# Issuing the value products of two attention heads together, into the two halves of TensorE's columns, in a two-layer hybrid backbone

## The chip, the cores and the metric

The kernel runs on one core of a Trainium2 chip. The metric is the device time of one execution in microseconds (us), as the median of several executions. All data is in HBM at the start and the output is in HBM at the end. Engines are called as in the profile: PE is TensorE's matrix multiply, PEld its weight load, DVE is VectorE, ACT is ScalarE, POOL is GpSimd, SP is SyncE, which here issues nearly all DMAs.

## What is computed

The reference is two layers of a backbone over 256 context and 256 latent tokens, width 1024, all in float32. Each layer mixes tokens in four parallel groups of four heads or channels (an mLSTM, latent attention "mla", windowed attention "swa", a linear recurrence) behind one input projection and before one output projection. Layer 0 then has a dense SwiGLU, layer 1 a mixture of eight experts, two per token. A conditioning vector gives shifts, scales and gates (`ada_w`). The part that matters here is the attention of the two middle groups:

```python
def block_attention(q, k, v):          # mla: 4 heads, blocks of 128 queries
    s = jnp.einsum('bhqd,bhkd->bhqk', qblk, k).astype(F32) * scale
    p = jax.nn.softmax(s, axis=-1)
    return jnp.einsum('bhqk,bhkd->bhqd', p.astype(v.dtype), v)
...
def swa_mixer(...):                    # swa: 4 heads, 2 groups of keys and values, window 128, a sink
    p = softmax_with_sink(s, sink_h[:, :, None, None, None]).astype(vl.dtype)
    o = (jnp.einsum('bhgnqk,bhnkd->bhgnqd', p[..., :KL], vb)
         + jnp.einsum('bhgnqk,bhkd->bhgnqd', p[..., KL:], vc))
```

Context queries see 256 keys, latent queries see 512. Layer 0 has outputs for all 512 tokens, layer 1 for the 256 latent ones only. Each head has 64 values per token.

## The kernel before, in words

Time goes through the program in this order: the start with the first modulation; the mixer of layer 0 (input projection, mLSTM, attention); its output projection (`w_out`); the dense SwiGLU (`ffn`); the mixer of layer 1; its `w_out`; the experts (`moe`), which stream their weights in 333 loads of 1024 KB.

**Attention** is one list of items, built by `items` (L819): one item is one head and one block `t` of 128 queries, with `w` keys (256 for t = 0, 1 and 512 for t = 2, 3). The four mla heads and then the four swa heads make 32 items in layer 0 (`full`) and 16 in layer 1 (t = 2, 3 only). The list runs head by head, and the blocks within a head. `attend` (L824) goes over the list as a software pipeline. In iteration i it issues

- `scores` (L831) of item i: the product of queries and keys into a bank of PSUM (L835; for swa a mask is added by a product with the identity, L838), then the softmax: maximum and sign on DVE (L842, L844), exponential with its sum on ACT (L849), reciprocal on DVE (L853), normalisation on POOL (L854);
- `turn` (L857) of item i - 3: PE transposes the probabilities P in pieces of 128 x 128 (L860), and ACT (odd i, L863) or DVE (even i, L865) copies them out of PSUM as PT;
- `value` (L868) of item i - 4: `w / 128` products add up one head's output. The weights are the head's values (128 keys x 64), the moving operand is PT (128 keys x 128 queries), and the result has 64 partitions.

```python
c, p = h // 2, 64 * (h % 2)
...
nc.tensor.matmul(ob[p:p + 64, t * 128:(t + 1) * 128], lhsT=q["head"][2](s), rhs=q["PT"][:, s * 128:(s + 1) * 128],
                 start=(s == 0), stop=(s == w // 128 - 1))
```

An even head writes partitions 0 to 63 of bank `ob`, that is, it uses columns 0 to 63 of the array; an odd head uses columns 64 to 127 and the other partitions of the same bank. After the last block of an odd head, `emit_y` (L588) splits the pair's output into a high and a low part for `w_out`.

**What stands beside it.** `mixer` (L1258) advances the mLSTM generator once per iteration of `attend` in layer 0 and twice in layer 1: decays (L735, L738 on PE, L742 on ACT), products (L752 on PE, L757 on DVE), values (L770 on PE). The mLSTM's end (L801 to L816, with transposes on PE at L809) waits in the program until attention is done. In layer 0 `tick` also lets a background generator `ada` go on, which loads `ada_w` (L335, tile `adaw`, on SP) and multiplies it (L347, L358). The tile framework orders each engine's instructions from these by priority and readiness, so a group of products can be cut by other work.

**Buffers.** P and PT come from one pool tag `t2` (34 buffers in layer 0, 33 in layer 1). The score and transpose banks have the tag A (4 banks); the banks of `value` and of the mLSTM have the tag B (3 banks in layer 0, 4 in layer 1).

A matrix product of plain float32 operands is one instruction in the program and two records in the trace, each with its own weight load.

Of the kernel before, what the change touches and what calls it, by code (L numbers as in the profile page):

```python
# [130 lines left out]
class Net:  # L131
# [685 lines left out]

    def items(self, i0, full, heads, sink=None):

        return [dict(i0=i0, h=h, head=hd, t=t, w=256 if t < 2 else 512, sink=sink, last=t == 3)  # L820
                for h, hd in enumerate(heads) for t in ((0, 1, 2, 3) if full else (2, 3))]

    def attend(self, items, full):

        nc, mp = self.nc, self.mp
        V = nc.vector
        c0 = 0 if full else 256
        obs = {}

        def scores(q):  # L830
            qT, kT, _ = q["head"]  # L831
            t, w, h, sink = q["t"], q["w"], q["h"], q["sink"]
            b = self.bank("A")
            loc = sink is not None and t >= 2
            nc.tensor.matmul(b[:, :w], lhsT=qT[:, t * 128:(t + 1) * 128], rhs=kT[:, :w], start=True, stop=not loc)  # L835
            if loc:
                o = 5 - t
                nc.tensor.matmul(b[:, o * 128:(o + 1) * 128], lhsT=self.ident,  # L838
                                 rhs=self.C("swa_m0" if t == 2 else "swa_m1"), start=False, stop=True)
            nm = mp.tile([128, 4], F32, name="nm", tag="nm", bufs=8)  # L840
            m, sm = nm[:, 0:1], nm[:, 1:2]
            V.tensor_reduce(m, b[:, :w], axis=AX.X, op=OP.max)  # L842
            if sink is None:
                V.tensor_scalar(m, m, -1.0, None, op0=OP.mult)  # L844
            else:
                sk = sink[:, h:h + 1]
                V.tensor_scalar(m, m, sk, -1.0, op0=OP.max, op1=OP.mult)
            P = q["P"] = self.T2("P")
            nc.scalar.activation(P[:, :w], b[:, :w], AF.Exp, bias=m, accum_out=sm)  # L849
            if sink is not None:  # L850
                nc.scalar.activation(nm[:, 2:3], m, AF.Exp, bias=sk)
                V.tensor_tensor(sm, sm, nm[:, 2:3], op=OP.add)
            V.reciprocal(sm, sm)  # L853
            nc.gpsimd.tensor_scalar(P[:, :w], P[:, :w], sm, 1.0, op0=OP.mult, op1=OP.mult)  # L854

        def turn(q, i):
            w = q["w"]  # L857
            b = self.bank("A")
            for s in range(0, w, 128):
                nc.tensor.transpose(b[:, s:s + 128], q["P"][:, s:s + 128], self.ident)  # L860
            pt = q["PT"] = self.T2("PT")
            if i % 2:
                nc.scalar.activation(pt[:, :w], b[:, :w], AF.Copy)  # L863
            else:
                V.tensor_copy(pt[:, :w], b[:, :w])  # L865

        def value(q):
            i0, h, t, w = q["i0"], q["h"], q["t"], q["w"]  # L868
            c, p = h // 2, 64 * (h % 2)
            if (i0, c) not in obs:  # L870
                obs[i0, c] = self.bank("B")
            ob = obs[i0, c]
            for s in range(w // 128):
                nc.tensor.matmul(ob[p:p + 64, t * 128:(t + 1) * 128], lhsT=q["head"][2](s), rhs=q["PT"][:, s * 128:(s + 1) * 128],  # L874
                                 start=(s == 0), stop=(s == w // 128 - 1))
            if q["last"] and p:
                self.emit_y(i0 + c, ob, c0)

        n = len(items)
        for i in range(n + 4):  # L880
            if i < n:
                scores(items[i])
            if 0 <= i - 3 < n:
                turn(items[i - 3], i)
            if i >= 4:
                value(items[i - 4])
            yield

    def rope(self, dst, x, parts, t0, nf, tmp):
# [980 lines left out]
```

## Time and profile before

| | us |
|---|---|
| median of 3 runs | 2014.39 (2011.48 to 2016.26) |
| the profiled execution | 2016.45 |
| its span, first to last instruction | 2014.7 |
| PE busy | 1876.2 (93% of the span), 10051 records |
| DVE, ACT, POOL busy | 918.4, 767.2, 85.3 |

The profile's busy times are those of one execution. A busy PE is not one at its peak: each record lasts from its start to a modelled end, and records overlap, so what a group of products costs is read from the distance between starts. [...] Attention lies between about 202 and 369 us (layer 0) and between 956 and 1028 us (layer 1).

### The profile page before, as it was taken

To read this page: it belongs to the slowest core of one execution; us is meant where nothing else is said; L and a number is where in the kernel's file an instruction comes from. 1 tells how busy PE (TensorE), PEld (TensorE's weight loads), DVE (VectorE), ACT (ScalarE), POOL (GpSimd) and SP (SyncE) were. 2 spreads that over 40 slices of the span, in tenths; PEclk is the share of its full clock that TensorE was granted. 3 is DMA by queue.
4 is the path that set the end of the run, shared out by engine and by line. 5 is a ranking of instruction groups with operands and counts; after the bars stand their busy time and mean duration, and the time that the engine had idled before them with its cause. 6 is when DMAs were issued, how large, how long until landed. Compare 5 with 4: busy or idle time off the path is not lost.

```text
span 2014.7 us, 26293 instructions
## 1 busy us (share of the span) xinstructions
PE 1876.2 (93%) x10051; PEld 1235.0 (61%) x10051; DVE 918.4 (46%) x1678; ACT 767.2 (38%) x1331; POOL 85.3 (4%) x121
## 2 busy tenths in 40 slices
PE   6999999989999999888988999789999989899988
PEld 3777455678888888667686886454454444444443
DVE  3556334453433434675567965333324333333323
ACT  3745433253223233654547854232322222323221
POOL 0210111000000000210100000000000000000000
PEclk8999899989999999888998989999999989999999
DMA  8543356412323233331045969999999989999997
GB/s 276 181 136 110 126 193 204 152 63 95 96 93 96 92 97 92 102 85 48 1 166 201 363 225 380 405 408 409 401 376 349 410 321 380 409 401 372 409 405 300
DMA packets 190958, 474.73 MB, mean 236 GB/s; under 512 B 18596, under 2 KB 81768, under 8 KB 190824
## 3 DMA queue, kind: packets, MB, share of 16 engines
q1 hardware_dynamic: 190456, 472.76, 64.2%
q8 instruction: 81, 1.33, 0.3%
q14 instruction: 53, 0.43, 0.1%
q10 hardware_dynamic: 368, 0.21, 0.0%
HBM read 471.88 MB, written 1.05 MB: 235 GB/s over the span
## 4 chain that ended last, share of the span: by engine, by line
PE 63%; DMA 5%; DVE 5%; ACT 3%; issue 2%; DVEq 0%; SPq 0%; ACTq 0%
PE bankA L1572 16%; PE bankA L528 7%; PE bankA L527 7%; PE bankA L526 7%; PE bankA L1567 6%; PE bankA L1568 5%; PE bankA L1566 5%; DMA w<-in_moe_w_dram 5%; DVE wl L210 2%; ACT wh L209 1%; PE bankA L1531 1%; PE bankA L1602 1%; PE bankA L835 1%; PE bankB L874 1%; PE bankA L1714 1%
## 5 line engine op out<-in xcount | busy, mean ns | idle before, releaser
L210 DVE TENSOR_TENSOR wl<-w,wh 128x1024 fp32r<-128x1024 f32 x222 | 263.9, 1222 | 257.8 <-ACT wh L209 245.7
L209 ACT ACTIVATE wh<-w 128x1024 fp32r<-128x1024 f32 x222 | 225.7, 1053 | 156.7 <-DMA w<-in_moe_w_dram 126.7
L1572 PE MATMUL bankA<-w,xl 128*32 128x256 f32 (+3 forms) x1784 | 228.4, 452 | 15.0 <-DMA w<-in_moe_w_dram 15.0
L1572 PEld LDWEIGHTS bankA<-w,xl 128*32 128x32 f32 (+1 forms) x1784 | 83.7, 124 | 134.3 <-issue 96.5
L1567 PE MATMUL bankA<-wl,xe 128*128 128x512 f32 x336 | 140.7, 419 | 19.2 <-DVE wl L210 19.2
L1566 PE MATMUL bankA<-wh,xe 128*128 128x512 f32 x336 | 129.0, 425 | 14.8 <-ACT wh L209 14.4
L1568 PE MATMUL bankA<-wh,xe 128*128 128x512 f32 x336 | 136.5, 406 | 0.0
L1572 PE MATMUL bankA<-w,ut 128*32 128x256 f32 (+1 forms) x792 | 116.4, 490 | 0.8 <-DMA w<-in_moe_w_dram 0.8
L1650 ACT ACTIVATE sg<-bankA 128x512 f32<-128x512 f32 (+2 forms) x45 | 23.1, 533 | 196.6 <-PE bankA L1572 159.1
L1566 PEld LDWEIGHTS bankA<-wh,xe 128*128 128x128 f32 x336 | 61.7, 194 | 54.4 <-ACT wh L209 28.8
L1567 PEld LDWEIGHTS bankA<-wl,xe 128*128 128x128 f32 x336 | 65.9, 196 | 44.0 <-DVE wl L210 29.7
L1567 PE MATMUL bankA<-wl,uh 128*128 128x512 f32 x168 | 68.8, 409 | 9.4 <-DVE wl L210 9.4
L1653 DVE TENSOR_TENSOR sg<-bankA,sg 128x512 f32<-128x512 f32 (+2 forms) x45 | 27.0, 612 | 108.7 <-PE bankA L1572 89.0
L1572 PEld LDWEIGHTS bankA<-w,ut 128*32 128x32 f32 (+1 forms) x792 | 36.6, 122 | 63.9 <-issue 56.5
L1568 PEld LDWEIGHTS bankA<-wh,xe 128*128 128x128 f32 x336 | 66.0, 196 | 13.9
L528 PE MATMUL bankA<-uh,w2l 128*128 128x512 f32 x176 | 70.2, 399 | 0.0
L528 PE MATMUL bankA<-hh,wgl 128*128 128x512 f32 x176 | 70.2, 399 | 0.0
L527 PE MATMUL bankA<-hl,wgh 128*128 128x512 f32 x176 | 69.3, 394 | 0.0
L527 PE MATMUL bankA<-ul,w2h 128*128 128x512 f32 x176 | 69.3, 394 | 0.0
L526 PE MATMUL bankA<-uh,w2h 128*128 128x512 f32 x176 | 69.0, 392 | 0.0
L526 PE MATMUL bankA<-hh,wgh 128*128 128x512 f32 x176 | 69.0, 392 | 0.0
L347 PE MATMUL bankC<-adaw,stat 128*32 128x512 f32 x352 | 67.3, 617 | 1.5 <-DMA adaw<-in_ada_w_dram 1.5
(489 smaller groups left out, 3679.1 us busy)
## 6 DMA issues: line engine op xcount, KB each, us to landing
w<-in_moe_w_dram SPq DMA_DIRECT2D x286, 1024.0 KB, 10.1
adaw<-in_ada_w_dram SPq DMA_DIRECT2D x96, 512.0 KB, 4.8
xT<-in_moe_w_dram SPq DMA_DIRECT2D x47, 1024.0 KB, 9.2
wa<-in_ffn_w_dram SPq DMA_DIRECT2D x22, 512.0 KB
wg<-in_ffn_w_dram SPq DMA_DIRECT2D x22, 512.0 KB, 3.5
w<-in_ffn_w_dram SPq DMA_DIRECT2D x20, 512.0 KB, 3.4
wo<-in_w_out_dram SPq DMA_DIRECT2D x12, 512.0 KB, 3.5
wU<-in_w_in_dram SPq DMA_DIRECT2D x4, 512.0 KB
```

The costliest lines, as they stand in the source:

```text
L209: nc.scalar.activation(h, src, AF.Copy)
L210: ins = nc.vector.tensor_tensor(lo[:, q:q + m], src, h.bitcast(F32), op=OP.subtract)
L347: mark(nc.tensor.matmul(b[32 * q:32 * q + 32], lhsT=self.stat[:, j], rhs=rs[j][:, h * 512:(h + 1) * 512], start=(i == 1), stop=(i == 7)))
L526: t.matmul(out, lhsT=whi, rhs=hhi, start=start, stop=False)
L527: t.matmul(out, lhsT=whi, rhs=hlo, start=False, stop=False)
L528: t.matmul(out, lhsT=wlo, rhs=hhi, start=False, stop=stop)
L1566: t.matmul(b, lhsT=x[0], rhs=hi[:, c], start=start, stop=False)
L1567: t.matmul(b, lhsT=x[0], rhs=lo[:, c], start=False, stop=False)
L1568: t.matmul(b, lhsT=x[1], rhs=hi[:, c], start=False, stop=stop)
L1572: t.matmul(out[0][n * s:n * s + n, 0:h], lhsT=x, rhs=w[:, s * h:(s + 1) * h], start=start, stop=stop)
L1650: nc.scalar.activation(g[:, 0:h], b[:, 0:h], AF.Silu)
L1653: V.tensor_tensor(g[:, 0:h], b[:, 0:h], g[:, 0:h], op=OP.mult)
```

## The change

The list of items goes by pairs of heads (0 and 1, then 2 and 3), within a pair by blocks, and within a block by the two heads. `value` takes both heads of a pair at once, in odd iterations only: it issues their products in turns, one of the lower and one of the upper half of the columns. So the first item of a pair has its products one iteration later than before, the second one as before.

```diff
-        return [dict(i0=i0, h=h, head=hd, t=t, w=256 if t < 2 else 512, sink=sink, last=t == 3)
-                for h, hd in enumerate(heads) for t in ((0, 1, 2, 3) if full else (2, 3))]
+        return [dict(i0=i0, h=h, head=heads[h], t=t, w=256 if t < 2 else 512, sink=sink, last=t == 3)
+                for c in range(2) for t in ((0, 1, 2, 3) if full else (2, 3)) for h in (2 * c, 2 * c + 1)]
...
-        def value(q):
-            i0, h, t, w = q["i0"], q["h"], q["t"], q["w"]
-            c, p = h // 2, 64 * (h % 2)
+        def value(qs):
+
+            i0, h, t, w = (qs[1][x] for x in ("i0", "h", "t", "w"))
+            c = h // 2
             if (i0, c) not in obs:
                 obs[i0, c] = self.bank("B")
             ob = obs[i0, c]
             for s in range(w // 128):
-                nc.tensor.matmul(ob[p:p + 64, t * 128:(t + 1) * 128], lhsT=q["head"][2](s), rhs=q["PT"][:, s * 128:(s + 1) * 128],
-                                 start=(s == 0), stop=(s == w // 128 - 1))
-            if q["last"] and p:
+                for p, q in zip((0, 64), qs):
+                    nc.tensor.matmul(ob[p:p + 64, t * 128:(t + 1) * 128], lhsT=q["head"][2](s), rhs=q["PT"][:, s * 128:(s + 1) * 128],
+                                     start=(s == 0), stop=(s == w // 128 - 1))
+            if qs[1]["last"]:
                 self.emit_y(i0 + c, ob, c0)
...
-            if i >= 4:
-                value(items[i - 4])
+            if i >= 4 and i % 2:
+                value(items[i - 5:i - 3])
```

Two lines are added, so the lines behind L872 move by two; the products are at L876 in the changed kernel.

The order of PE's instructions shows what becomes of it. First layer 1, between the transposes of one swa item and the next value products. `bankA` rows at L835, L838 and L860 are scores, mask and transposes; `qT,kT` and `v,E` are the mLSTM's; `PT,swv` are value products. Before:

```order
L860 MATMUL bankA_7993<-c_base,P 128x128 x4
L874 MATMUL bankB_8000<-PT,swv 64x128 x4
L752 MATMUL bankB_8005<-qT_7302,kT_7146 128x256
L770 MATMUL bankB_8009<-v,E_7728 128x65 x2
L770 MATMUL bankB_8009<-v,E_7729 128x65
L770 MATMUL bankB_8009<-v,E_7728 128x65 x2
L770 MATMUL bankB_8009<-v,E_7729 128x65
L770 MATMUL bankB_8009<-v,E_7731 128x65
L835 MATMUL bankA_8022<-swk_7166,swT_7151 128x512
L838 MATMUL bankA_8022<-c_mix,c_base 128x128
L860 MATMUL bankA_8034<-c_base,P 128x128 x4
L874 MATMUL bankB_8000<-PT,swv 64x128 x4
```

The same place now:

```order
L860 MATMUL bankA_7993<-c_base,P 128x128 x4
L752 MATMUL bankB_8000<-qT_7302,kT_7146 128x256
L770 MATMUL bankB_8004<-v,E_7728 128x65 x2
L770 MATMUL bankB_8004<-v,E_7729 128x65
L770 MATMUL bankB_8004<-v,E_7728 128x65 x2
L770 MATMUL bankB_8004<-v,E_7729 128x65
L770 MATMUL bankB_8004<-v,E_7731 128x65
L835 MATMUL bankA_8017<-swk_7166,swT_7156 128x512
L838 MATMUL bankA_8017<-c_mix,c_base 128x128
L860 MATMUL bankA_8029<-c_base,P 128x128 x4
L876 MATMUL bankB_8036<-PT,swv 64x128 x8
```

Two runs of four value products have become one run of eight, in which lower and upper half take turns; the rest of the row order is the same.

Second, the end of attention in layer 0, where the background's products (`adaw`) and the output projection (`woh`, `wol`) cut in. Before:

```order
L860 MATMUL bankA_3046<-c_base,P 128x128 x2
L358 MATMUL bankC_2908<-c_base,adar 128x4 x4
L860 MATMUL bankA_3046<-c_base,P 128x128 x2
L526 MATMUL bankA_3144<-yh_2171,woh 128x512
L874 MATMUL bankB_2858<-PT,swv 64x128 x4
L527 MATMUL bankA_3144<-yl_2172,woh 128x512
L347 MATMUL bankC_3057<-adaw,stat 32x512 x2
L874 MATMUL bankB_2858<-PT,swv 64x128 x4
L528 MATMUL bankA_3144<-yh_2171,wol 128x512
```

And now:

```order
L860 MATMUL bankA_3022<-c_base,P 128x128 x3
L876 MATMUL bankB_2888<-PT,swv 64x128 x8
L358 MATMUL bankC_2906<-c_base,adar 128x4 x4
L860 MATMUL bankA_3046<-c_base,P 128x128 x4
L347 MATMUL bankC_3053<-adaw,stat 32x512 x2
L876 MATMUL bankB_2888<-PT,swv 64x128 x3
L347 MATMUL bankC_3053<-adaw,stat 32x512 x2
L876 MATMUL bankB_2888<-PT,swv 64x128 x5
L526 MATMUL bankA_3144<-yh_2171,woh 128x512
```

The last pair's eight products are cut into a run of three and one of five, and the output projection's first product has moved behind them.

## Rows read from the trace of the kernel before

**Rows 1.** By stretch: us, busy PE, PEld, DVE, ACT, POOL (records), clock, DMA share, GB/s.

```profile
200.00:230.00 30.00, 28.13 (x108) 13.13 (x110) 9.59 (x31) 16.29 (x47) 4.01 (x7) 0.83 0.20 70
230.00:380.00 150.00, 150.00 (x855) 81.11 (x852) 57.89 (x191) 46.01 (x139) 17.71 (x29) 1.00 0.60 198
380.00:420.00 40.00, 40.00 (x170) 29.71 (x170) 19.72 (x36) 12.61 (x25) 0.00 (x0) 1.00 0.32 99
956.00:1028.00 72.00, 71.91 (x426) 51.60 (x425) 38.21 (x126) 33.88 (x102) 12.92 (x20) 0.97 0.00 1
...
1400.00:2014.70 614.70, 563.25 (x2879) 282.60 (x2877) 209.58 (x235) 159.69 (x199) 0.00 (x0) 0.98 0.98 378
```

**Rows 2.** The chain that ended last, inside layer 1's attention: start us, us, what.

```profile
1011.73 0.44 PE bankA L860 x4
1012.17 1.02 PE bankB L874 x8
```

**Rows 3.** The same chain, behind attention: the experts' first weights.

```profile
1039.76 8.88 DMA w<-in_moe_w_dram
```

**Rows 4.** PE in order of time at full clock: start us, us, instruction, records.

```profile
1011.57 0.60 PE L860 MATMUL bankA<-c_base,P 128*128 128x128 f32 x4
1012.10 1.09 PE L874 MATMUL bankB<-PT,swv 128*64 128x128 f32 x8
1013.12 1.13 PE L752 MATMUL bankB<-qT,kT 64*128 64x256 f32 x4
...
1014.18 1.12 PE L835 MATMUL bankA<-swk,swT 128*128 128x512 f32 x2
1015.14 0.39 PE L838 MATMUL bankA<-c_mix,c_base 128*128 128x128 f32 x2
```

**Rows 5.** The same view: a short run of value products in layer 0.

```profile
211.85 0.65 PE L874 MATMUL bankB<-PT,vm 128*64 128x128 f32 x4
212.43 1.00 PE L752 MATMUL bankB<-qT,kT 64*128 64x512 f32 x1
```

**Rows 6.** The same view: the experts' products in quarters, then in halves, of the columns.

```profile
1307.13 1.06 PE L1572 MATMUL bankA<-xT,xl 128*32 128x128 f32 x32
...
1401.20 1.94 PE L1572 MATMUL bankA<-w,xl 128*64 128x512 f32 x8
1402.96 1.89 PE L1572 MATMUL bankA<-xT,xl 128*64 128x512 f32 x8
1404.68 2.24 PE L1572 MATMUL bankA<-w,xl 128*64 128x512 f32 x12
```

**Rows 7.** Line L874, all run: duration ns min/median/max, starts; then PE's waits before it.

```profile
L874 PEld LDWEIGHTS bankB<-PT,vm x160: 132/137/230, 211.8 to 998.1; 128*64 128x64 f32 x160
L874 PE MATMUL bankB<-PT,vm x160: 272/273/477, 211.9 to 998.2; 128*64 128x128 f32 x160
...
  issue: 8.8, 39
  ACT E L742: 1.1, 3
  DVE nm L853: 0.8, 1
  DVE hss L803: 0.8, 1
  ACT P L849: 0.3, 1
  ACT den L773: 0.2, 1
```

**Rows 8.** Line L865, all run: the copies of PT on DVE.

```profile
L865 DVE COPY PT<-bankA x24: 405/680/693, 211.6 to 1024.5; 128x512 f32<-128x512 f32 x16, 128x256 f32<-128x256 f32 x8
```

**Rows 9.** Waits of SP's DMA queue, 200 to 440 us: for whom, us in total, times, longest.

```profile
SPq L335 <- PE bankC L347: 135.1, 36, 24.6
...
SPq L335 <- DMA adaw<-in_ada_w_dram: 4.9, 3, 2.0
```

## The prediction
> **What bounds the kernel now.** First I read busy time by stretch, to see which engine sets the pace where the value products stand. In layer 0's attention PE is busy for 150.00 of 150 us at full clock, while DVE, ACT and POOL are busy for 57.89, 46.01 and 17.71 us; in layer 1's it is 71.91 of 72 us, with the others at 38.21 or less [rows 1]. A busy PE can be a waiting one, so I looked next at the chain of waits. In layer 1 it runs from one PE piece to the next without a gap (1011.73 + 0.44 = 1012.17), and the value products are links of it [rows 2]. What is cut out of PE there should therefore shorten the time, if what follows moves along. It does: behind attention the chain goes to the experts' first weight load, issued at 1039.76 us [rows 3]. In attention itself the DMA share is 0.00, and from 1400 us to the end it is 0.98 [rows 1]. So the experts' stream begins when layer 1's mixer lets it, and the end moves with its beginning. Layer 0's attention is followed by more PE-bound work (40.00 of 40 us) [rows 1].
>
> **What a run of value products costs.** The time in order, read from start to start: a run of eight records (four products) takes 1013.12 - 1012.10 = 1.02 us [rows 4], a run of four takes 212.43 - 211.85 = 0.58 us [rows 5]. So a record costs (1.02 - 0.58) / 4 = 0.110 us, a product of two records 0.220 us, and each run pays 0.14 us besides. Another 0.09 us falls on the instruction ahead of a run: four transposes take 1012.10 - 1011.57 = 0.53 us, of which 0.44 us are theirs [rows 4]. The trace has 320 records in two groups of 160, of which one is shown [rows 7], that is, 160 products: 96 in layer 0, 64 in layer 1. In the order of the kernel before they stand in 51 runs (35 and 16). They cost 160 x 0.220 + 51 x 0.14 = 42.3 us of PE.
>
> **Do two halves run at once?** No value products do so now, since a run keeps to one half. The experts' products show it: eight records of 512 columns in halves of 64 take 1402.96 - 1401.20 = 1.76 us, or 0.44 us for two [rows 6], while records of 512 columns over the whole width take (1015.14 - 1014.18) / 2 = 0.48 us each, a switch included [rows 4]. Two halves cost what one costs. They use the same order as the change (halves inside, accumulation outside, one bank). At 128 columns, the width of the value products, 32 records in quarters take 1.06 us; without the last one's 0.27 us that is 0.113 us for four at once [rows 6], against 0.110 us for one value record. So I take 0.220 us for a step of two products; its upper bound from that row is 0.226 us, and from no overlap at all 0.440 us.
>
> **The change, part by part.**
> *Products.* In the order of the changed kernel the 160 products stand in 33 runs (23 and 10). Halves alternate, so a run of n takes n/2 steps, rounded up: where other work cuts a run at an odd place, one product stays alone. Counted over the runs that is 55 steps in layer 0 (48 would be the least) and 34 in layer 1 (32). Saved are 41 and 30 steps: 9.0 us and 6.6 us.
> *Runs.* 12 and 6 runs fewer at 0.14 us: 1.7 and 0.8 us. The 0.09 us ahead of a run may go too, or stay with the neighbours that now meet: 0 to 1.6 us for 18 runs. I take half, 0.5 and 0.3 us, since half of the neighbours shown in the order (transposes next to a 64-row mLSTM product) are of unlike shapes still.
> *Sum on PE.* 11.2 us in layer 0 and 7.7 us in layer 1.
> *Other engines.* The same softmax, normalisation and copy instructions go in another order; nothing is added, I cost it at nothing. Their cover is a PE that is busy almost twice as long as any of them, or longer [rows 1]. SP's order moves one small router load past two output-weight loads: nothing.
> *Waits.* The first item of each pair waits one iteration longer for its products, and the PT tile lives as much longer, one more of 34 (33) buffers. Who could wait is the PE: the upper half's product needs the second item's PT, and the queue behind it is all of PE. That copy always falls on DVE now (even iterations) and takes 0.69 us at 512 columns [rows 8]. Before, none of PE's waits ahead of value products ends with a copy of PT [rows 7]. Now in the order the second item's transposes have a mLSTM product, seven small ones, the scores, the mask and four transposes between them and the run: the last three alone take 0.96 us and more [rows 4]. I cost it at nothing; if the cover were gone it would be the slower case below.
> *What gets through.* In layer 1 all of it, 7.7 us, since the chain there is PE alone. In layer 0 ACT is busy for 16.29 of the first 30 us and the clock is at 0.83 there [rows 1], and SP waited three times, 4.9 us in all, for a load of the background to land [rows 9]; a PE that is 11.2 us shorter meets such limits oftener. Bounds are 0 and 11.2 us. I take four fifths, 9.0 us, nearer to the full amount because SP waited 135.1 us for PE to free those buffers and so follows PE [rows 9].
>
> Sum: 7.7 + 9.0 = 16.7, say 17 us. The profiled execution took 2016.45 us (span 2014.7), which would become 1999.4; it is 2.1 us above the median of the runs, 2014.39, from which the same 17 us give **1997.4 us**.
>
> **The rivals.**
> 1. *Layer 0 gives nothing back.* There the end of the mixer would be set by the background's loads or by the softmax chain, and PE's time would turn into waiting. For it: the late loads; DMA share 0.60. Against it: SP waits for PE, not PE for SP [rows 9], and PE is busy throughout. Left is layer 1: 2014.4 - 7.7 = 2006.7 us. Chance 0.14.
> 2. *The halves don't run at once* at this size, so the change does not do what it says. Left are the 18 runs: 2.5 us, with the entries up to 4.1; some 2011.4 us, which is within 0.2%. Against it stand rows 6. Chance 0.06.
> 3. *A wait takes the place of the products* (slower). If PE stands before each upper half until the copy of PT is there, 24 pairs wait. The gain is gone at 18.9 / 24 = 0.79 us a pair. A run right behind its transposes would wait for the last record (0.27 us, as a value record), the copy (0.69) and one DVE instruction of the same size ahead of it (0.69): 1.65 x 24 - 18.9 = 20.7 us slower, 2035 us. Against it: the order keeps other products between, except at the very end of layer 1, where one pair stands close. Chance 0.04.
> 4. *The weight loads come out from behind the products* (slower). Each record has a load of 0.137 us [rows 7]. Now they are hidden, for a record comes every 0.110 us. If two halves in turn kept the loads from running ahead, a step would cost 2 x (0.110 + 0.137) = 0.494 us: 89 x 0.494 + 33 x 0.14 = 48.6 us against 42.3, 6.3 us slower, 2020.7 us. Rows 6 speak against it: loads of the same kind stand there and two records come in 0.44 us. Chance 0.02. [...]
>
> **How the numbers follow.** A measurement of this kernel tells about 0.2%, 4 us, from no change (the three runs lie 4.8 us apart). Forecast 0.74, rivals 0.14, 0.06, 0.02 and 0.04. Faster by over 0.2% are the forecast and the first rival, less a little for sizes that come out small: 0.86. Within 0.2% is the second and that little: 0.08. Slower are the third and fourth: 0.06. The forecast's own bounds: if everything gets through with all entries and one run of products less at half clock, 11.2 + 7.7 + 0.8 + 0.5 = 20.2 us, 1994.2; with half of the spread of the runs below it, 1991.5. The upper end takes in the first rival with some of the spread: 2008.5. A wider clock difference is not priced: only the first 30 us of layer 0's attention and the first of layer 1's are below 1.00, and they hold few value products.
>
> **What would show it.** Right: value records in pairs some 0.01 us apart, so a run of 16 records (eight products) takes about 1.02 us from start to start; layer 1's attention is shorter by 7 to 8 us and the experts' first load comes earlier by the sum of both layers. Layer 0's `w_out` begins 9 to 11 us earlier, without longer waits before L347. Wrong: runs of 16 records in 1.9 us (rival 2) or more (rival 4); waits of PE ahead of L876 that end with a copy of PT (rival 3); L347 that waits for `adaw` (rival 1). A stretch before the experts that shortens as forecast, with an end that does not move, would show that the experts' stream is not set by its beginning, and the prediction would be wrong there.

## The result, and the profile after

The changed kernel takes **1993.03 us** (median of 20 runs, 1984.77 to 2010.2), the kernel before, beside it, 2017.01 us (20 runs, 2008.53 to 2025.35). The ratio is 0.9891, 95% interval [0.9873, 0.9909]: 22 us faster (18 to 26). The forecast was 17 us and 1997.4 us. A second measurement with other kernels gave 0.9874 [0.9838, 0.991].

The profiled execution took 1993.35 us, with a span of 1991.5 us. Busy time by stretch, for [rows 1]: us, busy PE, PEld, DVE, ACT, POOL (records), granted clock as a share of full clock, DMA share, GB/s.

```profile
198.90:230.00 31.10, 30.26 (x161) 16.30 (x160) 14.22 (x46) 19.13 (x59) 5.13 (x9) 1.00 0.40 135
230.00:350.00 120.00, 120.00 (x744) 62.08 (x743) 49.35 (x163) 39.56 (x123) 16.47 (x27) 1.00 0.63 213
936.00:1001.00 65.00, 64.91 (x430) 45.92 (x429) 38.70 (x132) 33.08 (x102) 12.89 (x20) 0.96 0.00 1
1400.00:1991.50 591.50, 541.67 (x2767) 273.29 (x2767) 203.24 (x229) 154.37 (x192) 0.00 (x0) 0.98 0.98 377
```

PE still sets the pace in both attentions (120.00 of 120 and 64.91 of 65 us). What is new is the clock of the first row: 1.00, where it was 0.83 over 200 to 230 us [rows 1].

The chain that ended last, inside layer 1's attention and behind it, for [rows 2, 3]: start us, us, what.

```profile
990.27 0.44 PE bankA L860 x4
990.71 1.02 PE bankB L876 x16
...
1011.49 8.54 DMA w<-in_moe_w_dram
```

Sixteen records now take the 1.02 us that eight took, and the experts' first load is issued at 1011.49 us instead of 1039.76. Of these 28 us, 3 are there before layer 0's attention begins (198.90 us against 201.86), where the change does not reach; in the second profile that beginning is at 203.75 us. The same on PE in order of time, for [rows 4]:

```profile
958.12 0.60 PE L860 MATMUL bankA<-c_base,P 128*128 128x128 f32 x4
958.65 1.09 PE L876 MATMUL bankB<-PT,vm 128*64 128x128 f32 x16
959.68 0.48 PE L752 MATMUL bankB<-qT,kT 64*128 64x256 f32 x1
```

All value products of a group, and the idle time before them until what, for [rows 7]. It is that of the weight loads (PEld), as the trace's list of waits by engine shows:

```profile
L876 PEld LDWEIGHTS bankB<-PT,vm x160: 132/137/138, 211.4 to 974.8; 128*64 128x64 f32 x160
L876 PE MATMUL bankB<-PT,vm x160: 272/273/325, 211.4 to 974.9; 128*64 128x128 f32 x160
...
  issue: 7.1, 25
  DVE den L774: 0.8, 1
  PE bankA L838: 0.2, 1
  ACT den L773: 0.2, 1
```

One record and one load last as long as before (medians of 273 and 137 ns), and no wait ends with a copy of PT. Summed from each value record's start to the next start on PE, the products cost 26.5 us in layer 0 and 16.3 us in layer 1 before, 15.4 and 8.9 us now: 42.8 - 24.3 = **18.5 us** less. From the first score to the last value product, layer 0's attention went from 166.8 to 151.2 us, layer 1's from 71.3 to 63.9 us. So layer 0 is 15.6 us shorter, of which its value products explain 11.1.

SP's waits between 190 and 420 us, for [rows 9]:

```profile
SPq L335 <- PE bankC L347: 114.3, 34, 14.7
...
SPq L335 <- DMA adaw<-in_ada_w_dram: 4.8, 5, 1.5
```

SP waits less for PE (135.1 before) and no longer for its loads (4.9 before).

**Where the rest of layer 0's gain is.** PE at the start of layer 0's attention in the kernel before; what stands in the gap of this copy is [rows 5].

```profile
209.10 0.38 PE L860 MATMUL bankA<-c_base,P 128*128 128x128 f32 x2
211.22 0.70 PE L835 MATMUL bankA<-mkT,mqT 96*128 96x256 f32 x2 [1.74 <-ACT P L849]
...
214.21 1.87 PE L358 MATMUL bankC<-c_base,adar 128*128 128x4 f32 x8
```

The same place in the changed kernel:

```profile
206.58 1.12 PE L752 MATMUL bankB<-qT,kT 64*128 64x512 f32 x2
207.63 0.44 PE L860 MATMUL bankA<-c_base,P 128*128 128x128 f32 x2
207.91 0.95 PE L358 MATMUL bankC<-c_base,adar 128*128 128x4 f32 x8
209.13 1.07 PE L347 MATMUL bankC<-adaw,stat 128*32 128x512 f32 x8 [0.27 <-DVE mod L363]
210.13 1.12 PE L835 MATMUL bankA<-mkT,mqT 96*128 96x512 f32 x2
```

Before, a score (L835) waited 1.74 us for ACT to empty a bank, and from 212.7 to 222.9 us the granted clock was 0.50, the level that the expectations below call 1.2 GHz (the traces give it as a share alone): L358 took 1.87 us, where it takes 0.95 now. A window inside that stretch of the kernel before, columns as above:

```profile
213.00:222.80 9.80, 9.80 (x30) 4.34 (x28) 2.40 (x7) 1.80 (x5) 0.93 (x2) 0.50 0.01 3
```

In the changed kernel the first value products come one iteration later. The scheduler therefore put L752, L358 and L347 ahead of the score, the bank is free when PE gets there, and the clock stays at 1.00. At a granted clock of 0.50, 10.2 us hold an estimated 5.1 us of work (L358's 1.87 us against 0.95 speak for it); with the stop that is 6.8 us that the prediction had not priced. Not all of it is gain beside the products. Half a microsecond of the slow work is a run of value products (the four records at 216.96 us take 1.05 us to the next start, 0.58 at full clock) and is counted with them already, and the changed kernel's PE still stands for 0.84 us in this attention (1.74 before). Net it is some 5.5 us by this count; the attention itself leaves 15.6 - 11.1 = 4.5 us.

Two theories were to be told apart. **Step theory**: all of the gain is steps and runs (18 to 18.5 us); the clock at the start differs by chance. **Start theory**: some 5 to 7 us come from the later place of the first value products alone, which takes away the stop and with it the fall of the clock.

### The profile page after: what moved, and what is told of

Same layout as the page of the kernel before. It is cut to its first block, busy times and chain, and to the rows that moved or that the text cites. A ratio compares the mean times of both kernels' runs of the same rounds, so it can differ in the third digit from the quotient of the medians.

```text
span 1991.5 us, 26295 instructions
## 1 busy us (share of the span) xinstructions
PE 1860.3 (93%) x10051; PEld 1226.9 (62%) x10051; DVE 918.0 (46%) x1678; ACT 766.1 (38%) x1331; POOL 85.3 (4%) x121
## 3 DMA queue, kind: packets, MB, share of 16 engines
HBM read 471.88 MB, written 1.05 MB: 237 GB/s over the span
## 4 chain that ended last, share of the span: by engine, by line
PE 65%; DVE 5%; DMA 5%; ACT 3%; issue 2%; DVEq 0%; SPq 0%; ACTq 0%
PE bankA L1574 16%; PE bankA L527 7%; PE bankA L526 7%; PE bankA L528 7%; PE bankA L1569 6%; PE bankA L1570 6%; PE bankA L1568 5%; DMA w<-in_moe_w_dram 5%; DVE wl L210 2%; ACT wh L209 1%; PE bankA L1533 1%; PE bankA L1604 1%; PE bankA L835 1%; PE bankA L1545 1%; PE bankA L1716 1%
## 5 line engine op out<-in xcount | busy, mean ns | idle before, releaser
L347 PE MATMUL bankC<-adaw,stat 128*32 128x512 f32 x352 | 68.3, 607 | 1.9 <-DMA adaw<-in_ada_w_dram 1.6
```

Of the source, the lines that this page charges most:

```text
L347: mark(nc.tensor.matmul(b[32 * q:32 * q + 32], lhsT=self.stat[:, j], rhs=rs[j][:, h * 512:(h + 1) * 512], start=(i == 1), stop=(i == 7)))
```

## The experiments

Each kernel ran beside the kernel before on the same chip (2017.9, 2019.69, 2018.43 and 2018.31 us in the four sessions, on three chips). "Cost" is that of the value products in layer 0 and layer 1, "stop" the longest one of PE above 0.6 us in the first 20 us of layer 0's attention, "at 0.50" the time at that granted clock in its first 30 us, all from the profiled execution.

| kernel | steps / runs | cost, us | stop, us | at 0.50, us | ratio to before |
|---|---|---|---|---|---|
| before | 160 / 51 | 26.5 + 16.3 | 1.7 | 10.2 | 1 |
| order_only | 159 / 48 | 26.9 + 15.9 | 1.5 | 17.1 | 0.9987 [0.9972, 1.0002] |
| layer1_only | 130 / 45 | 26.5 + 8.9 | 1.7 | 10.2 | 0.9972 [0.9957, 0.9987] |
| no_slack | 104 / 48 | 19.1 + 11.0 | 1.5 | 13.7 | 0.9965 [0.9935, 0.9994] |
| late_single | 159 / 49 | 26.0 + 15.6 | none | 0 | 0.9964 [0.9942, 0.9986] |
| layer0_only | 119 / 39 | 15.4 + 16.3 | none | 0 | 0.9931 [0.9908, 0.9954] |
| head_after_head | 140 / 34 | 19.7 + 12.6 | none | 0 | 0.9914 [0.9888, 0.9939] |
| early_first | 90 / 33 | 16.1 + 8.9 | 1.5 | 10.2 | 0.9913 [0.9882, 0.9945] |
| stop_13 | 89 / 33 | 15.4 + 8.9 | 2.9 | 6.8 | 0.9921 [0.9896, 0.9947] |
| stop_fifth | 90 / 34 | 16.8 + 8.9 | 1.0 | 0 | 0.9920 [0.9892, 0.9949] |
| stop_8 | 89 / 33 | 15.4 + 8.9 | none | 0 | 0.9875 [0.9837, 0.9912] |
| after_again | 89 / 33 | 15.4 + 8.9 | none | 0 | 0.9874 [0.9838, 0.991] |
| stop_fourth | 90 / 34 | 15.7 + 8.9 | none | 0 | 0.9865 [0.9848, 0.9883] |

**order_only**: the new list of items, the products one head at a time at the old place.

```diff
-                for h, hd in enumerate(heads) for t in ((0, 1, 2, 3) if full else (2, 3))]
+                for c in range(2) for t in ((0, 1, 2, 3) if full else (2, 3)) for h in (2 * c, 2 * c + 1)]
```

> Items in the new order, each item's products issued alone as before. Step theory (what counts is that a step does two halves at once, 0.220 us a step, 0.14 us a run): 159 steps and 48 runs against 160 and 51, so 0.6 us less at most: no change within 0.2%. Rival (the new order of the items is what helps, by another pace of the softmax or a kinder clock at the start of layer 0's attention): a gain of several us, up to the 24 us measured for the whole change.

Measured: 2.6 us less, within an interval that reaches to no change. The order of the items alone gives little or nothing (6 us at most by the interval); the stop and the slow stretch stay.

**head_after_head**: pairs, but four products of the lower half and then four of the upper.

```diff
-            for s in range(w // 128):
-                for p, q in zip((0, 64), qs):
+            for p, q in zip((0, 64), qs):
+                for s in range(w // 128):
```

> Both heads' products issued together, but all of the lower half before all of the upper one. Step theory: halves meet only where one head ends and the other begins, at most once in a run: 140 steps and 34 runs against 160 and 51, so 20 x 0.220 + 17 x 0.14 = 6.8 us less, and 2.4 us less if even that meeting does not overlap. Rival (issuing a pair together is enough, since fewer switches of shape or a deeper queue bring the gain): about as much as the whole change, 20 us or more.

Measured: 17 us faster (12 to 23), which at first sight speaks for another cause than the overlap. But the products' cost fell only by 42.8 - 32.3 = 10.5 us, more than counted, since the halves overlap here even without turns. PE in order of time, one pair of this kernel and what follows:

```profile
957.10 1.58 PE L876 MATMUL bankB<-PT,vm 128*64 128x128 f32 x16
958.61 1.77 PE L770 MATMUL bankB<-v,E 128*128 128x65 f32 x14
```

The run takes 1.51 us; two separate runs of eight would take 2.04 [rows 4], turns 1.03. The rest goes with the start: no stop and no slow stretch here either, and layer 0's attention is 12.0 us shorter (154.8 us) with products that cost 6.8 us less there, which leaves 5.2 us.

**layer0_only** and **layer1_only**: the change in one layer (`if full:` or `if not full:` around the new list and the paired issue, the old ones otherwise).

> The whole change in layer 0 alone. Step theory: 41 steps and 12 runs less, 10.7 us, 11.2 with the entries; with the half-clock stretch at the start of attention gone for good, as in the profile of the change, some 14 us. Rival (layer 0's end is set by the background's loads or the softmax): no gain. Rival (the gain stands in the clock alone): a gain with no fewer microseconds in the value products.

> The whole change in layer 1 alone. Step theory: 30 steps and 6 runs less, 7.4 us, 7.7 with the entries, if the experts' stream passes an earlier start on in full. If the experts give some of it back, as the profile of the change suggests (its first weight load is 28 us earlier, its end 23 us), 3 to 7 us. Rival (the experts' end does not depend on their beginning): no change.

Measured: 14 us (9 to 19) and 5.6 us (3 to 9). Their attentions take 151.1 us and 63.9 us, to 0.1 us those of the full change, so the two layers add up. For layer 0 alone the interval still holds its 11.2 us of steps and runs; the profile tells more, an attention 15.7 us shorter (166.8 before) with products that cost 11.1 us less.

**late_single**: the kernel before with every product one iteration later. It has no pairs and no overlap.

```diff
-        for i in range(n + 4):
+        for i in range(n + 5):
...
-            if i >= 4:
-                value(items[i - 4])
+            if i >= 5:
+                value(items[i - 5])
```

> The kernel before with one edit: every item's products with the values are issued one iteration later, still one head at a time and in the old order of items. In PE's order they stand in 49 runs and 159 steps (before 51 and 160), and the mLSTM's product L752 now stands ahead of the transposes for which PE waited at the start of layer 0's attention. Step theory (all of the gain comes from halves that run at once and from fewer runs): 0.5 us, the time of before, ratio 0.9985 to 1.000. Start theory (part of the gain in layer 0 comes from the later place of the first value products: the 2 us stop of PE at about 209 us is filled, and the clock does not fall behind it): 5 to 7 us faster, ratio 0.9965 to 0.9975, layer 0's attention 160 to 162 us instead of 167 to 170, no stretch at 1.2 GHz in its first 20 us. Chance theory (the stretch at 1.2 GHz comes and goes by itself): as the step theory in the time, with or without the stretch in the profile.

Measured: 7.3 us faster (3 to 12), with products that cost 41.6 us, only 1.2 less than before. Layer 0's attention takes 161.4 us, as the start theory had it, though two later stretches (from 234.4 and from 299.2 us, 3.4 us each) ran at a granted clock of 0.50. L752 stands where the changed kernel has it:

```profile
209.83 1.12 PE L752 MATMUL bankB<-qT,kT 64*128 64x512 f32 x2
210.88 0.44 PE L860 MATMUL bankA<-c_base,P 128*128 128x128 f32 x2
211.16 0.95 PE L358 MATMUL bankC<-c_base,adar 128*128 128x4 f32 x8
```

**early_first** and **after_again**: the changed kernel with only the first two items issued singly at the old place, beside the changed kernel itself.

```diff
-            if i >= 4 and i % 2:
+            if full and i in (4, 5):
+                value(items[i - 4:i - 3])
+            elif i >= 4 and i % 2:
                 value(items[i - 5:i - 3])
```

> The changed kernel with one edit: only the first two items of layer 0 have their products singly, at the place of the kernel before; all others go by pairs. PE's order has 23 runs and 56 steps in layer 0 (the changed kernel 23 and 55), and the first value products stand ahead of L752 again. Step theory: 0.2 us slower than the changed kernel, that is, some 20 to 22 us faster than before. Start theory: PE stops for about 2 us at 207 to 211 us again, the clock falls to 1.2 GHz for 10 to 17 us behind it, and the kernel is 5 to 7 us slower than the changed one, some 15 us faster than before (ratio 0.992 to 0.993).

> The changed kernel once more, for its place beside the others on the same chip and a second profile. Step theory and start theory alike: 18 to 24 us faster than before. Start theory: again no stretch at 1.2 GHz in the first 20 us of layer 0's attention; chance theory: it may stand there this time.

Measured: 2002.95 and 1993.36 us. This edit costs 9.6 us between the medians; by the count of steps it should cost 0.2. Layer 0's attention took 160.3 and 152.2 us. PE at the start in early_first:

```profile
213.62 0.38 PE L860 MATMUL bankA<-c_base,P 128*128 128x128 f32 x2
215.47 0.70 PE L835 MATMUL bankA<-mkT,mqT 96*128 96x512 f32 x1 [1.47 <-ACT P L849]
```

The stop is back, and behind it the low clock, 0.63 on the mean (a window of its start, columns as above):

```profile
216.00:230.00 14.00, 14.00 (x49) 6.03 (x48) 3.70 (x11) 3.08 (x9) 1.57 (x3) 0.63 0.10 22
```

After_again has neither, as in the first profile. With this the step theory falls as the whole account.

**no_slack**: a pair's products right in the iteration in which its second item is transposed; the price of the third rival.

```diff
-            if i >= 4 and i % 2:
-                value(items[i - 5:i - 3])
+            if i >= 4 and i % 2 == 0:
+                value(items[i - 4:i - 2])
```

> The changed kernel with one edit: a pair's products are issued in the iteration in which the second item is transposed, so its copy of PT stands right ahead of them. PE's order has 48 runs and 104 steps (the changed kernel 33 and 89, before 51 and 160), because the scheduler puts one product of the lower half early and the others behind other work. If PE does not have to wait for the copies: 56 steps of 0.220 us and 3 runs of 0.14 us, 12.7 us faster than before, ratio 0.9937. If it waits as the third rival of the prediction has it, 0.7 to 1.0 us at each of 24 pairs (17 to 24 us): 4 to 11 us slower than before, and PE's waits ahead of L876 end with a copy of PT.

Measured: 7 us faster (1 to 13). The products cost 30.1 us, 12.7 less than before and to 0.1 us what steps and runs give. PE's waits ahead of L876 come to this one line:

```profile
PE bankB L876 <- ACT PT L863: 0.2, 1, 0.2
```

So even without slack PE doesn't stand before the copy; the scheduler puts other products between, which shows as more runs. Its time gained less than the 12.7 us of steps and runs, though the interval reaches there. The start had a stop of 1.5 us and 13.7 us at a clock of 0.50, and the mean granted clock over its runs was 0.956 (0.960 before); more was not followed.

**stop_fourth** and **stop_fifth**: does a stop of PE bring the clock down by itself? The changed kernel, with ACT's exponential of one early item repeated.

```diff
             P = q["P"] = self.T2("P")
+            for _ in range(8 if full and q is items[3] else 0):
+                nc.scalar.activation(P[:, :w], b[:, :w], AF.Exp, bias=m)
```

> The changed kernel with one edit: in layer 0 the exponential of the fourth item (index 3) is computed eight times more into the same tile, some 2.9 us of ACT (eight times 0.36 us), near the place where the kernel before had its stop. PE's order keeps 24 runs and 56 steps in layer 0 (the changed kernel 23 and 55, 0.4 us). The scheduler puts this exponential behind those of the fifth and sixth item, so a stop of PE, if it comes, comes some us later than in the kernel before. Stop theory (a stop of PE of 1.5 us or more in this stretch is followed by a fall of the clock): a stop of 1 to 3 us, then 1.2 GHz for some 10 us, and 5 to 10 us slower than the changed kernel, ratio 0.990 to 0.993. Order theory (the clock follows from what stands in PE's order there, not from the stop): at most the stop itself, 0 to 3 us slower than the changed kernel, no stretch at 1.2 GHz. If PE finds no stop above 1 us, both expect the time of the changed kernel, ratio 0.987 to 0.989.

> The same with the exponential of the fifth item (index 4, 512 keys) computed twelve times more, some 6.8 us of ACT (twelve times 0.57 us), of which about 4.2 us fall into a stretch in which ACT is idle in the changed kernel. PE's order is that of the changed kernel up to the first pair. Stop theory: a stop of 1 to 4 us at about 212 to 218 us, 1.2 GHz for some 10 us behind it, 6 to 10 us slower than the changed kernel, ratio 0.990 to 0.993. Order theory: the stop alone, 1 to 4 us slower, no stretch at 1.2 GHz. Without a stop above 1 us both expect the time of the changed kernel.

Measured: the first made no stop and tells nothing of the question (its time is that of the changed kernel). The second (12 times, `items[4]`) made three short ones, the longest

```profile
220.64 1.12 PE L752 MATMUL bankB<-qT,kT 64*128 64x512 f32 x2 [1.01 <-ACT E L742]
```

and no slow stretch in its profile. It took 6 to 9 us more than the changed kernel (0.9920 against 0.9891 and 0.9874), of which its layer 0's attention shows 3 to 4 (155.3 us against 151.2 and 152.2); the rest stays unexplained. The profiled execution took 1995.05 us, the shortest of six, and the median is 1999.12, so the profile need not show all that the median holds. It is a miss for the stop theory, or too small a stop.

**stop_13** and **stop_8**: one larger stop at the old place, by POOL, and a control with the same order on PE.

```diff
             nc.gpsimd.tensor_scalar(P[:, :w], P[:, :w], sm, 1.0, op0=OP.mult, op1=OP.mult)
+            for _ in range(13 if full and q is items[1] else 0):
+                nc.gpsimd.tensor_scalar(P[:, :w], P[:, :w], 1.0, 1.0, op0=OP.mult, op1=OP.mult)
```

> The changed kernel with one edit: in layer 0 POOL multiplies the probabilities of the second item by 1.0 thirteen times more (0.45 us from one to the next). PE's order is that of the changed kernel but for one row: the second item's transposes stand behind L358 instead of ahead of it. They now wait for POOL until about 210.7 us on the clock of the profile of after: a stop of PE of about 2 us, at the place in the order where the kernel before stopped, with nothing else changed. Stop theory: the clock falls to 1.2 GHz within some us behind the stop, for 10 to 17 us, and the kernel is 6 to 10 us slower than the changed one, ratio about 0.991 to 0.993. Order theory (the clock follows from what PE does there, not from the stop): no stretch at 1.2 GHz, the 2 us of the stop alone, ratio 0.988 to 0.990.

> The control: the same with eight multiplications more. PE's order is the same as with thirteen, but POOL is done at about 208.5 us, before PE comes to the transposes, so that PE has no stop of more than 0.6 us there. Both theories: no stretch at 1.2 GHz in the first 20 us of layer 0's attention, and the time of the changed kernel, ratio 0.987 to 0.989.

PE in stop_13, and then in stop_8:

```profile
211.19 1.05 PE L358 MATMUL bankC<-c_base,adar 128*128 128x4 f32 x8
215.17 0.69 PE L862 MATMUL bankA<-c_base,P 128*128 128x128 f32 x2 [2.93 <-POOL P L856]
215.79 1.94 PE L347 MATMUL bankC<-adaw,stat 128*32 128x512 f32 x8
```

```profile
209.33 1.05 PE L358 MATMUL bankC<-c_base,adar 128*128 128x4 f32 x8
210.85 0.44 PE L862 MATMUL bankA<-c_base,P 128*128 128x128 f32 x2 [0.47 <-POOL P L856]
211.22 1.07 PE L347 MATMUL bankC<-adaw,stat 128*32 128x512 f32 x8
```

Behind a stop of 2.93 us L347 takes 1.94 us instead of 1.07, and the clock is at 0.50 for 6.8 us from 213.3 us on, a moment within the stop. A window of stop_13, columns as above:

```profile
213.40:220.10 6.70, 4.93 (x15) 1.47 (x15) 0.49 (x2) 0.78 (x2) 2.63 (x6) 0.50 0.18 43
```

The kernels took 2005.47 and 1995.11 us: the stop and what follows cost 10.4 us between the medians, of which layer 0's attention shows 6.2 in the profiles (159.5 against 153.3). The other 4 us are not placed: the two profiled executions lie only 2.0 us apart (1996.93 and 1994.9 us), for in stop_8's the experts' beginning ran at 0.50 for 30.7 us, in stop_13's for 17.1. The order of PE is the same in both. So at this place a stop of this size (2.93 us) brought the clock down to 0.50 with nothing changed in the order, as one profile of each kernel shows.

In the first 30 us of layer 0's attention, over all kernels: the six with one stop of about 1.5 us or more have the slow stretch behind it, the eight without have none.

It is no rule for every place. Just ahead of this attention PE stops for 1.47 to 1.51 us in all 14 kernels, for DVE (L669). In nine of them 3.4 us at a clock of 0.50 stand behind that stop, in five none: in layer0_only, stop_fifth, order_only and stop_13 and in the kernel before, whose row comes first here, with that of the changed kernel, which has the fall:

```profile
195.72 0.46 PE L669 MATMUL bankB<-c_base,bb 64*128 64x64 f32 x4 [1.49 <-DVE bb L664]
192.77 0.46 PE L669 MATMUL bankB<-c_base,bb 64*128 64x64 f32 x4 [1.48 <-DVE bb L664]
```

And four times, later in this attention, 3.4 us at 0.50 came with no stop in the 10 us ahead: in late_single (234.4 and 299.2 us), layer1_only (264.6) and stop_13 (298.7). What else decides about the clock no run here shows.

## Why the prediction was right, and where it was not

- **What bounds the kernel**: right. PE is busy in both attentions before and after, but for 1.74 us before and 0.84 us after in layer 0's, and the end moved with the experts' first load (28 us earlier, the end 23; in the second profile 24 and 25).
- **What a run costs**: right. 160 products in 51 runs were put at 42.3 us and cost 42.8; 89 steps and 33 runs come by the same sizes to 24.2 us and cost 24.3.
- **Do two halves run at once**: right. The two records of a step start 5 to 8 ns apart, the steps 0.10 to 0.11 us; a run of 16 records takes 1.03 us from start to start, where 1.02 was forecast. Rival 2 is out.
- **The entries** (0.5 and 0.3 us) are too small to be told apart.
- **Layer 0 gives nothing back** (rival 1): out. Layer 0 alone gave 14 us (9 to 19), and L347's weight loads wait 0.9 us for `adaw` between 195 and 420 us, where they waited 1.5 before.
- **Waits** (rival 3): none in the changed kernel, 0.2 us even in no_slack. The cover that was named, products between the second item's transposes and the run, holds. The list under [rows 7], on which part of this rested, is of the weight loads' waits alone; it says nothing of PE, which had no wait of its own ahead of value products, before or after.
- **Weight loads** (rival 4): 137 ns each, still hidden: a step of two records comes every 0.11 us.
- **Layer 1, 7.7 us**: right in the profile (7.4 us shorter) and within the interval of layer1_only (3 to 9 us).
- **Layer 0, "What gets through"**: this is the step that was wrong. It took four fifths of 11.2 us, 9.0, because ACT is busy for 16.29 of 30 us and the clock is 0.83 there. Layer 0's attention became 15.6 us shorter, more than the 11.1 us of its products, so the 2 us were taken off for nothing. And what was read as a limit on the gain was a loss that the change removes: ACT held a score bank, PE stopped for 1.7 us, and the clock fell to 0.50. The sentence "A wider clock difference is not priced" left out the term. It could have been read: 30 us at a clock of 0.83 are 5.1 us short of full clock [rows 1], with the stop at most 6.8. In layer 0's attention the start is worth 4.5 us in the changed kernel, 5.2 in head_after_head and 4.9 in late_single, each without the products' part; in the whole time late_single measures 7.3 and early_first against after_again 9.6 us, each to several us. ACT's share was read as a reason to take something off, where it was part of the loss.

Sum by what was measured: 18.5 us of products and some 5 of the start, 23 to 24 us (the two attentions are 15.6 + 7.4 = 23.0 us shorter), against 22 (18 to 26) and 25 (18 to 33) in the two measurements. The forecast's 17 us is low by the start and by the fifth taken off. That 1993.03 us lies inside the forecast's bounds is owed to their width: with all that the prediction added up, its best case was 1994.2 us, and only half of the spread of the runs took the bound below that (4.8 / 2 = 2.4 us, so 1991.8 and not the 1991.5 that it says).

In the first profile after, some 5 us were lost again in the experts' beginning, where 30.7 us ran at a clock of 0.50 (17.1 before). In the second profile it was 17.1 us and nothing was lost, and late_single, which has no pairs, shows 30.7 us too; so it is no part of the change.

No version faster than the changed kernel was found. What is left of uneven runs there is 9 steps, 2 us.

## What to carry to other kernels

Two products that use 64 columns each cost one here if they stand next to each other and go to different halves (16 records in 1.03 us, 8 in 1.02 before); count steps and runs in the order that the scheduler really gives, since cuts at odd places leave products alone. When a change moves work in time, read the stretch it leaves and not only its own cost: a stop of PE of 1.7 us that other work can fill was worth about a fifth of the whole gain (some 5 of 23 us), because the granted clock fell to 0.50 behind it. A low clock in a stretch is a question (did PE stop just before, and would a change remove that?) before it is a bound; a stop of that length is no sure sign, for behind L669's (1.47 to 1.51 us) the clock was at 0.50 in nine kernels of 14.

## What was not expected of the hardware

In head_after_head the two halves of the columns did not keep the order of the program between them. Eight records of the lower half stand there ahead of eight of the upper one. The starts in one run, in us after 957:

```
lower  0.098 0.258 0.367 0.476 0.585 0.694 0.804 0.913
upper                          0.591 0.751 0.860 0.969 1.079 1.188 1.297 1.406
```

The trace doesn't name the half; the two series are told apart by their equal steps of 0.109 us. If they are told apart rightly, the upper half began while three records of the lower one had not yet started. More than half of the products' gain came without any turns in the program (10.5 of 18.5 us).

The clock's fall is large for so short a stop. At the start of layer 0's attention six kernels with a stop of 1.5 to 2.9 us were at a clock of 0.50 for 6.8 to 17.1 us behind or from within it; with at most 1.0 us at once, none. Elsewhere the same length was followed by 3.4 us or by nothing (L669), and 3.4 us at 0.50 came four times without any stop.
